# A second group of seven products in each gate/up pair, with two of its weight sums made in DRAM

## The chip, the cores and the metric

The kernel runs on one core of a Trainium2 chip. The metric is device time in microseconds (us) of one launch. The kernel before takes 2517.18 us, the median of three runs from 2516.54 to 2518.18 us. All arithmetic is float32 in the sense that every matrix product is built from reduced-precision parts, as described below.

## The reference, cut to what matters

Two layers on 256 tokens with a width of 2048. The first layer is a Mamba-2 mixer, the second is attention with forget gates; each is followed by the same feed-forward block, and that block is what the change is about:

```
def swiglu(h, w_gate_up, w_down):
    g, u = jnp.split(h @ w_gate_up, 2, axis=-1)
    return (jax.nn.silu(g) * u) @ w_down
...
h = h + swiglu(rmsnorm(h, ffn_norm_w[layer]), w_gate_up[layer], w_down[layer])
```

`h` is 256 x 2048, `w_gate_up` is 2048 x 11264 (gate and up, 5632 columns each), `w_down` is 5632 x 2048, all float32. Each of the two layers has its own weights, so the block runs twice.

## The kernel before, in words

**Tiling.** Every weight is cut into blocks of 512 columns, and each block into groups of 512 rows (a k group: four k tiles of 128 rows, 1 MB). The 256 tokens are two halves of 128. For one k tile and one token half, TensorE does three products into the same PSUM bank: high part of the activation by high part of the weight, high by low, low by high. So a k group of one block costs 4 x 2 x 3 = 24 matmuls of 128x512, and of a pair of blocks (one gate block and its up block) 48.

**Splitting weights.** A loaded weight tile (`wraw`) is split by two engines: ScalarE writes the rounded high part (`whi`, `split_hi`, line 260), VectorE writes the remainder (`wlo`, `split_lo`, line 266). One such step, two k tiles by 512 columns, is called a piece here; it feeds 12 matmuls. There are four buffers each of `whi` and `wlo` (`SPL`), and the pieces are split three ahead of the one that TensorE multiplies, so the high part of a piece waits until TensorE has finished the piece four before it.

**Pairs and seven products.** `pair` (line 320) builds two blocks that share their activations. In the k groups named by `crossed`, the 2x2 arrangement (two token halves, two k tiles by two blocks) is computed with seven products in place of eight, by sums of weights and sums of activations: 7 x 2 x 3 = 42 matmuls in place of 48. The seven are called d, g, a, c, e, b, f. Four are held in PSUM banks of their own (d, a, c, e; tag `mis`, four banks in all), three go straight into the two blocks' accumulators (tag `acc`, also four banks in all). VectorE makes the sums of weights in place in `wraw` (line 384), four additions of 128x1024 per group, between the splits. Afterwards `parts` (lines 677 to 686) combines d, a, c and e on VectorE, `gate` adds them to the left block's accumulators and applies SiLU, and `up` does the same with the right block, multiplies, and transposes the result into an activation slot.

**Order around the change.** A feed-forward block has eleven gate/up pairs; each has four k groups, and k group 2 is the crossed one. The order within a pair is left 0, left 1, right 0, right 1, the seven products of group 2, left 3, right 3. A pair's left accumulators are the banks that the next pair's left block takes first.

**Planner.** Everything but the matmul stream (`parts`, `gate`, `up`, transposes, the mixers) is a task that `Flow` advances at points between matmuls, when its own clock says that its inputs are ready and that ScalarE and VectorE are not more than 4 us behind. `finish` places what is left of a task at once: the next pair's left block forces the previous `gate` (lines 493 to 495), and the first product that needs a bank of its own forces all urgent and middle tasks (line 413). Each engine then executes its instructions strictly in the order in which they were placed.

**Loads.** Sync (SP) issues one 1 MB DMA per k group and block into one of three `wraw` buffers (`RAW`), after the last split that reads the buffer. GpSimd (POOL) computes a power for each normalisation (line 526) and issues the mixers' own DMAs (lines 819, 919, 1117, 1120); nothing else.

Of the kernel before, what the change touches and what calls it, by code (L numbers as in the profile page):

```python
# [17 lines left out]
P = 128  # L18
# [21 lines left out]
RAW = 3  # L40
SPL = 4

# [137 lines left out]
class Unit:  # L180


    def __init__(self, blk, kg, src, width, pieces):
        self.blk, self.kg, self.src, self.width, self.pieces = blk, kg, src, width, pieces
        self.raw = None


class Block:
# [3 lines left out]
    def __init__(self, xs, done, fills=None, wcol=None):  # L192
        self.xs, self.done, self.fills, self.wcol = xs, done, fills, wcol
        self.units, self.ps, self.task = [], None, None


class Cross:
# [8 lines left out]
    ORDER = "dgacebf"  # L206

    def __init__(self, left, right, parts):
        self.left, self.right, self.parts, self.ps = left, right, parts, {}


class Group:

# [6 lines left out]
def kernel(ctx: ExitStack, tc: tile.TileContext, xT_d, x_d, cols_d, rows_d, wdt_d, win_d,  # L220
# [84 lines left out]

    def wide(xs, src, done, fills=None, wcol=None):

        b = Block(xs, done, fills, wcol)
        for kg in range(len(xs)):
            b.units.append(Unit(b, kg, src[kg].rearrange("p (k n) -> p k n", n=NB), NB, [[0, 1], [2, 3]]))  # L310
        blocks.append(b)

    def narrow(xs, src, width, done, wcol=None):

        b = Block(xs, done, None, wcol)
        nk, step = KT * len(xs), NB // width
        b.units.append(Unit(b, 0, src, width, [list(range(a, min(a + step, nk))) for a in range(0, nk, step)]))
        blocks.append(b)

    def pair(xs, sources, done, fills, crossed, parts):  # L320


        both = [Block(xs, d, f) for d, f in zip(done, fills)]
        x = Cross(*both, parts)
        order, rights = [], []
        for kg in range(len(xs)):
            us = [Unit(b, kg, src[kg].rearrange("p (k n) -> p k n", n=NB), NB, [[0, 1], [2, 3]])
                  for b, src in zip(both, sources)]
            if kg in crossed:
                order += rights  # L330
                rights = []
                order.append(Group(x, us, xs[kg], kg == crossed[0], kg == crossed[-1]))
            else:
                for b, u in zip(both, us):
                    b.units.append(u)
                order.append(us[0])
                rights.append(us[1])
        blocks.append(order + rights)

# [7 lines left out]
    def load(u, apart=False, before=None):  # L347
        n = sum(len(p) for p in u.pieces)
        u.raw = wraw.tile([P, n, u.width], F32, tag="wraw", name=nm("wraw"))
        for ks in u.pieces if apart else [range(n)]:  # L350
            if before is not None:
                before(ks)
            nc.sync.dma_start(out=u.raw[:, ks[0]:ks[-1] + 1, :], in_=u.src[:, ks[0]:ks[-1] + 1, :])

    def split_piece(u, ks):
        n = len(ks)
        us = n * u.width / 1024
        ready = flow.work("V", 1.14 * us, flow.work("A", 0.95 * us, flow.at["E"]) + LAT)
        raw = u.raw[:, ks[0]:ks[0] + n, :]
        wcol = u.blk.wcol  # L360
        if u.width < NB:
            both = wspl.tile([P, n, 2, u.width], F32R, tag="whi", name=nm("whi"))
            if wcol is not None:
                nc.vector.tensor_tensor(out=raw, in0=raw, op=ALU.mult,
                                        in1=cols[:, wcol + ks[0]:wcol + ks[0] + n].unsqueeze(2).to_broadcast([P, n, u.width]))
            split(both[:, :, 0, :], both[:, :, 1, :], raw)
            return both, None, ready
        hi = wspl.tile([P, n, u.width], F32R, tag="whi", name=nm("whi"))
        lo = wspl.tile([P, n, u.width], F32R, tag="wlo", name=nm("wlo"))
        if wcol is None:  # L370
            split(hi, lo, raw)
        else:
            for i, k in enumerate(ks):
                split(hi[:, i, :], lo[:, i, :], raw[:, i, :], col(wcol + u.kg * KT + k))
        return hi, lo, ready

    def split_cross(x, name):

        (g, u) = (v.raw.rearrange("p (j i) n -> p i j n", i=2) for v in x.units)
        b11, b21, b12, b22 = g[:, 0], g[:, 1], u[:, 0], u[:, 1]  # L380

        def add(out, in0, in1):
            flow.work("V", 1.22, flow.at["E"])
            nc.vector.tensor_tensor(out=out, in0=in0, in1=in1, op=ALU.add)  # L384

        src = {"d": b21, "g": b11, "a": b21, "c": b22, "e": b21, "b": b22, "f": b12}[name]
# [3 lines left out]
        if name == "g":  # L390
            add(b22, b12, b22)
        if name == "c":
            add(b21, b12, b21)
        split_lo(hi, lo, src)
        ready = flow.work("V", 1.22, flow.work("A", 1.05, flow.at["E"]) + LAT)
        if name == "d":
            add(b21, b21, b22)
        if name == "c":
            add(b22, b11, b21)
        return hi, lo, ready  # L400

    def cross_step(group, name, parts):
# [20 lines left out]
        for p in range(2):  # L423
            xh, xl = a_of(0, p), a_of(1, p)
            nc.tensor.matmul(ps, lhsT=xh, rhs=hi[:, p, :], start=group.first and p == 0 and name not in own, stop=False)  # L425
            nc.tensor.matmul(ps, lhsT=xh, rhs=lo[:, p, :], start=False, stop=False)  # L426
            nc.tensor.matmul(ps, lhsT=xl, rhs=hi[:, p, :], start=False, stop=group.last and p == 1 and name not in own)  # L427
        if group.last and name == "e":
            spawn(x.parts(x))
        flow.work("E", STEP)  # L430
        flow.pump()

    def stream(pre_load, pre_split):
        pieces, units = [], []
        for b in blocks:
            for u in b.units if isinstance(b, Block) else b:
                if isinstance(u, Group):
                    pieces += [(u, n) for n in Cross.ORDER]
                    units += u.units
# [4 lines left out]
        loaded = [0]  # L444

        def load_to(n):
            while loaded[0] < min(n, len(units)):
                i = loaded[0]
                if i in pre_load:
                    pre_load[i]()  # L450
                load(units[i], i < 2, load_x0 if i == 0 else None)
                loaded[0] += 1

        def split_to(n):
            for i in range(len(parts), min(n, len(pieces))):
                u, ks = pieces[i]
                if isinstance(u, Group):
                    parts[i] = split_cross(u, ks)
                    if ks in "ef":
                        load_to(units.index(u.units["ef".index(ks)]) + 1 + RAW)  # L460
                    continue
                if i in pre_split:
                    pre_split[i]()
                parts[i] = split_piece(u, ks)
                if ks is u.pieces[-1]:
                    load_to(units.index(u) + 1 + RAW)

        load_to(RAW)
        split_to(SPL - 1)
        held = deque()  # L470
        for i, (u, ks) in enumerate(pieces):
# [8 lines left out]
            if u.width < NB:  # L480
                if b.ps is None:
                    b.ps = bank([2 * u.width, T])
                for j, k in enumerate(ks):
# [13 lines left out]
            last = u is b.units[-1] and ks is u.pieces[-1]  # L497
# [3 lines left out]
            for n, (j, t) in enumerate(order):  # L501
                k = u.kg * KT + ks[j]
# [3 lines left out]
                nc.tensor.matmul(b.ps[t], lhsT=xh, rhs=hi[:, j, :], start=k == 0, stop=False)  # L506
                nc.tensor.matmul(b.ps[t], lhsT=xh, rhs=lo[:, j, :], start=False, stop=False)  # L507
                nc.tensor.matmul(b.ps[t], lhsT=xl, rhs=hi[:, j, :], start=False, stop=k == nk - 1)  # L508
# [3 lines left out]
            if last:  # L512
                b.task = spawn(b.done(b.ps))
                if b.fills is not None:
                    b.fills.task = b.task
# [156 lines left out]
    def ffn_up(xs, r, gu_d, summed):  # L672
# [37 lines left out]
        for nb in range(NFB):  # L710
            x = [None]

            def took(y, x=x):
# [4 lines left out]
                 (None, acts[nb]), (2,), took)  # L718
# [312 lines left out]
    xs2, r2 = out_stage(ys, wout_d, C_F0, WOUT, summed=(2,))  # L1031
# [182 lines left out]
    xs4, r4 = out_stage(oT, wo_d, C_F1, (2,), summed=(2,))  # L1214
# [15 lines left out]
    pre_load = {i: (lambda i=i: load_x(i)) for i in range(4)}  # L1230
    pre_load[5] = late_loads
    pre_load[12] = load_h
# [5 lines left out]
    blocks[0].units[0].pieces = [[0], [1], [2, 3]]  # L1238
# [7 lines left out]
def _blocks(w):  # L1246
# [3 lines left out]
    w = w.reshape(k // 512, KT, P, n // NB, NB)  # L1250
# [13 lines left out]
def _layout(i):  # L1264
# [13 lines left out]
    def gu(w):  # L1278
        g, u = _blocks(w[:, :DFF]), _blocks(w[:, DFF:])
# [10 lines left out]
        "wout": _blocks(i["a_out_proj"][0]),  # L1290
        "gu0": gu(i["w_gate_up"][0]),
        "dn0": _blocks(i["w_down"][0]),
# [4 lines left out]
        "wo": _blocks(i["w_o"][0]),  # L1297
        "gu1": gu(i["w_gate_up"][1]),
        "dn1": _blocks(i["w_down"][1]),
# [21 lines left out]
```

## Time and profile before

| | |
|---|---|
| median of three runs | 2517.18 us |
| profiled execution, its own time | 2517.21 us |
| span in its profile | 2515.4 us |
| TensorE busy | 2502.9 us, 11542 matmuls |
| VectorE busy | 1938.8 us (77%) |
| ScalarE busy | 1370.1 us (54%) |
| DMA moved | 481.11 MB, 191 GB/s over the span |
| granted TensorE clock | 1.00 throughout |

A busy TensorE is one whose matmuls overlap, so busy time alone does not say that it runs at its fastest; the distance from one matmul's start to the next does. The launch takes about 1.8 us beyond the span.

### The profile page before, as it was taken

Reading aid. Unit: us, or ns where it says so; the run is one execution under the profiler, and the core shown is the slowest. Engines: PE = TensorE matmul, PEld = TensorE weight load, DVE = VectorE, ACT = ScalarE, POOL = GpSimd, SP = SyncE. Lnnn points to the kernel's source line nnn. Section 1 sums busy time; section 2 is a strip of 40 time slices with the busy share of each in tenths; the row PEclk is TensorE's granted clock in tenths of the full one; section 3 lists DMA queues with packets and bytes.
Section 4 is the critical chain, followed back from the end, with each engine's and each line's share of the span. In section 5 each row is a group of like instructions: output and inputs, shape, how many; then the busy total and the mean of one; then the engine's idle time right before and its main releaser. Section 6 shows DMA issues by size and latency. Waiting matters only on the chain.

```text
span 2515.4 us, 30043 instructions
## 1 busy us (share of the span) xinstructions
PE 2502.9 (100%) x11542; PEld 2076.0 (83%) x11542; DVE 1938.8 (77%) x2499; ACT 1370.1 (54%) x1733; POOL 39.5 (2%) x52
## 2 busy tenths in 40 slices
PE   9999999999999999999999999999999999999999
PEld 7888888887878888888888888888878888888887
DVE  7777777778788878788767667678887878879767
ACT  6665566555555555455545555655555555555544
POOL 0000000000000000000000000000000000000000
PEclk9999999999999999999999999999999999999999
DMA  7655455445554646465565555444555564645564
GB/s 269 223 175 174 178 182 203 167 168 196 186 203 168 218 167 223 178 217 184 181 216 187 200 175 203 163 168 170 182 182 203 184 215 169 219 167 206 200 230 150
DMA packets 68319, 481.11 MB, mean 191 GB/s; under 512 B 7600, under 2 KB 8256, under 8 KB 10576
## 3 DMA queue, kind: packets, MB, share of 16 engines
q1 hardware_dynamic: 66672, 468.64, 52.5%
q0 software_dynamic: 1504, 10.57, 1.0%
q8 instruction: 90, 1.47, 0.2%
q14 instruction: 53, 0.43, 0.0%
HBM read 477.00 MB, written 2.18 MB: 190 GB/s over the span
## 4 chain that ended last, share of the span: by engine, by line
PE 96%; DVE 3%; DMA 1%; ACT 0%; issue 0%; SPq 0%; ACTq 0%; DVEq 0%
PE acc L506 26%; PE acc L507 26%; PE acc L508 26%; PE mis L426 2%; PE mis L427 2%; PE mis L425 2%; PE acc L425 2%; PE acc L427 2%; PE acc L426 2%; PE mis L539 1%; DVE wlo L266 1%; PE mis L967 1%; DVE wraw L384 1%; PE mis L837 0%; DMA xraw<-in_xT_dram 0%; PE mis L973 0%
## 5 line engine op out<-in xcount | busy, mean ns | idle before, releaser
L266 DVE TENSOR_TENSOR wlo<-wraw,whi 128x1024 fp32r<-128x1024 f32 (+1 forms) x899 | 1079.7, 1220 | 349.1 <-ACT whi L260 341.2
L260 ACT CAST whi<-wraw 128x1024 fp32r<-128x1024 f32 (+1 forms) x902 | 929.4, 1049 | 740.4 <-PE acc L508 544.5
L506 PE MATMUL acc<-whi,xT 128*128 128x512 f32 x2816 | 1107.2, 393 | 0.5 <-ACT whi L260 0.4
L507 PE MATMUL acc<-wlo,xT 128*128 128x512 f32 x2816 | 1097.4, 390 | 1.0 <-DVE wlo L266 0.7
L508 PE MATMUL acc<-whi,xT 128*128 128x512 f32 x2816 | 1097.5, 390 | 0.0
L508 PEld LDWEIGHTS acc<-whi,xT 128*128 128x128 f32 x2816 | 528.9, 188 | 110.8
L507 PEld LDWEIGHTS acc<-wlo,xT 128*128 128x128 f32 x2816 | 529.4, 188 | 109.9 <-DVE wlo L266 2.6
L506 PEld LDWEIGHTS acc<-whi,xT 128*128 128x128 f32 x2816 | 529.3, 188 | 109.1 <-issue 1.2
L268 DVE SCALAR_TENSOR_TENSOR wlo<-wraw,cols,whi 128x512 fp32r<-128x512 f32 x192 | 134.6, 748 | 70.8 <-ACT whi L262 70.3
L262 ACT ACTIVATE whi<-wraw,cols 128x512 fp32r<-128x512 f32 x192 | 127.5, 717 | 72.2 <-PE acc L508 67.1
L384 DVE TENSOR_TENSOR wraw<-wraw,wraw 128x1024 f32<-128x1024 f32 x76 | 93.0, 1224 | 3.3 <-DMA wraw<-in_wout_dram 1.0
L384 DVE TENSOR_TENSOR wraw<-wraw 128x1024 f32<-128x1024 f32 x76 | 93.1, 1225 | 2.6
L426 PE MATMUL mis<-wlo,xS 128*128 128x512 f32 x228 | 89.5, 393 | 4.2 <-DVE wlo L266 4.2
L427 PE MATMUL mis<-whi,xS 128*128 128x512 f32 x228 | 88.7, 389 | 0.0
L425 PE MATMUL mis<-whi,xS 128*128 128x512 f32 x228 | 88.7, 389 | 0.0
L266 DVE TENSOR_TENSOR xT<-mis,xT 128x512 fp32r<-128x512 f32 x52 | 33.5, 686 | 37.2 <-ACT xT L260 37.2
L260 ACT CAST xT<-mis 128x512 fp32r<-128x512 f32 x52 | 27.9, 590 | 53.4 <-PE mis L539 53.4
L425 PE MATMUL acc<-whi,xT 128*128 128x512 f32 x144 | 56.1, 389 | 0.0
L427 PE MATMUL acc<-whi,xT 128*128 128x512 f32 x144 | 56.0, 389 | 0.0
L426 PE MATMUL acc<-wlo,xT 128*128 128x512 f32 x144 | 56.0, 389 | 0.0
L426 PEld LDWEIGHTS mis<-wlo,xS 128*128 128x128 f32 x228 | 42.8, 188 | 15.9 <-DVE wlo L266 7.3
L526 POOL TENSOR_TENSOR rs<-ms,mhalf 128x4 f32<-128x4 f32 (+1 forms) x27 | 30.2, 1119 | 1494.8 <-DVE ms L524 1494.5
(241 smaller groups left out, 1890.7 us busy)
## 6 DMA issues: line engine op xcount, KB each, us to landing
wraw<-in_gu_dram SPq DMA_DIRECT2D x176, 1024.0 KB, 4.9
wraw<-in_dn_dram SPq DMA_DIRECT2D x88, 1024.0 KB, 4.9
wraw<-in_win_dram SPq DMA_DIRECT2D x78, 1024.0 KB, 4.9
wraw<-in_wout_dram SPq DMA_DIRECT2D x32, 1024.0 KB, 5.0
wraw<-in_wq_dram SPq DMA_DIRECT2D x16, 1024.0 KB, 5.0
wraw<-in_wk_dram SPq DMA_DIRECT2D x16, 1024.0 KB, 4.9
wraw<-in_wv_dram SPq DMA_DIRECT2D x16, 1024.0 KB, 4.9
wraw<-in_wo_dram SPq DMA_DIRECT2D x16, 1024.0 KB, 4.9
```

Of the source, the lines that this page charges most:

```text
L260: nc.scalar.copy(out=hi, in_=src)
L262: nc.scalar.activation(hi, src, AF.Copy, scale=scal)
L266: nc.vector.tensor_tensor(out=lo, in0=src, in1=hi.bitcast(F32), op=ALU.subtract)
L268: nc.vector.scalar_tensor_tensor(out=lo, in0=src, scalar=scal, in1=hi.bitcast(F32), op0=ALU.mult, op1=ALU.subtract)
L384: nc.vector.tensor_tensor(out=out, in0=in0, in1=in1, op=ALU.add)
L425: nc.tensor.matmul(ps, lhsT=xh, rhs=hi[:, p, :], start=group.first and p == 0 and name not in own, stop=False)
L426: nc.tensor.matmul(ps, lhsT=xh, rhs=lo[:, p, :], start=False, stop=False)
L427: nc.tensor.matmul(ps, lhsT=xl, rhs=hi[:, p, :], start=False, stop=group.last and p == 1 and name not in own)
L506: nc.tensor.matmul(b.ps[t], lhsT=xh, rhs=hi[:, j, :], start=k == 0, stop=False)
L507: nc.tensor.matmul(b.ps[t], lhsT=xh, rhs=lo[:, j, :], start=False, stop=False)
L508: nc.tensor.matmul(b.ps[t], lhsT=xl, rhs=hi[:, j, :], start=False, stop=k == nk - 1)
L526: nc.gpsimd.tensor_tensor(out=r, in0=ms, in1=mhalf[:, :width], op=ALU.pow)
```

## The change

In ten of the eleven gate/up pairs of each feed-forward block, k groups 1 and 2 are both computed by seven products; in the last pair only group 2, as before. The order within a pair becomes left 0, right 0, group 1, left 3, group 2, right 3, and the order of the seven products f, d, c, a, e, g, b. The four banks of d, c, a and e are held from group 1 to group 2, and the left block is finished with group 2's product b.

Of the sums of weights in these groups, two (b22 + b12 and b22 + b21, 512 KB each) no longer come from VectorE. They are made in DRAM by GpSimd's queue: a DMA copies one part into a DRAM tile, a second DMA adds the other part to it; the group then loads five parts of 512 KB (f, d, c, a, g) in place of two of 1 MB, and VectorE makes the two remaining sums. `next_sum` is called with every eighth load in program order, and also where a load needs a sum that has not been made. All other weights are loaded in units of 512 KB as well, into six buffers in place of three; a buffer is given to the next load when all units before it are dead too. On the host, the k tiles of the paired weights are stored in the order 0, 2, 1, 3, so that a unit is contiguous. The activation sums are made for k groups 1 and 2.

```
-RAW = 3
+RAW = 6
+PACE = 8
...
 def pair(xs, sources, done, fills, crossed, parts, made=False):
...
+            us = [halves(b, kg, src[kg], ([0, 2], [1, 3])) for b, src in zip(both, sources)]
             if kg in crossed:
-                order += rights
-                rights = []
-                order.append(Group(x, us, xs[kg], kg == crossed[0], kg == crossed[-1]))
+                if not (made and kg > crossed[0]):
+                    order += rights
+                    rights = []
+                (b11, b21), (b12, b22) = us
+                if made:
+                    c, a = Sum(b22.src, b12.src), Sum(b22.src, b21.src)
+                    sums.extend((c, a))
+                    first = {"f": b12, "d": b21, "c": Unit(None, kg, c, NB, [1, 3]),
+                             "a": Unit(None, kg, a, NB, [1, 3]), "g": b11}
+                else:
+                    first = {"d": b21, "g": b11, "+": b22, "f": b12}
+                order.append(Group(x, first, xs[kg], kg == crossed[0], kg == crossed[-1]))
...
+        if made and len(crossed) > 1:
+            n = next(i for i in range(len(order) - 1, 0, -1) if isinstance(order[i], Group))
+            both[0].after = order.pop(n)
+            order.append(both[0].after)
         blocks.append(order + rights)
+
+    def next_sum(n=1):
+        for _ in range(n):
+            i = next((i for i, v in enumerate(sums) if not v.made), None)
+            if i is None:
+                return
+            for v in sums[i:i + 2]:
+                if v.tile is None:
+                    v.tile = dram.tile([P, 2, NB], F32, name=nm("wsum"))
+                    nc.gpsimd.dma_start(out=v.tile, in_=v.one)
+            nc.gpsimd.dma_start(out=sums[i].tile, in_=sums[i].other, accum_op=ALU.add)
+            sums[i].made = True
...
+        if group.cross.made:
+            place, dead = {"e": "c", "b": "c"}, {"f": "f", "c": "d", "a": "a", "g": "g", "b": "c"}
+            early, late = {}, {"c": ("c", "c", "d"), "e": ("c", "c", "g")}
...
+        def load_on():
+            while dead[0] < len(units) and units[dead[0]].dead:
+                dead[0] += 1
+            while loaded[0] < min(dead[0] + RAW, len(units)):
                 i = loaded[0]
                 if i in pre_load:
                     pre_load[i]()
-                load(units[i], i < 2, load_x0 if i == 0 else None)
+                if i % PACE == PACE - 1:
+                    next_sum()
+                load(units[i], i == 0, load_x0 if i < 2 else None)
                 loaded[0] += 1
...
-                 (None, acts[nb]), (2,), took)
+                 (None, acts[nb]), (1, 2) if nb < NFB - 1 else (2,), took, made=True)
...
-    xs2, r2 = out_stage(ys, wout_d, C_F0, WOUT, summed=(2,))
+    xs2, r2 = out_stage(ys, wout_d, C_F0, WOUT, summed=(1, 2))
-    xs4, r4 = out_stage(oT, wo_d, C_F1, (2,), summed=(2,))
+    xs4, r4 = out_stage(oT, wo_d, C_F1, (2,), summed=(1, 2))
...
+PAIRED = (0, 2, 1, 3)
```

## Rows read from the trace of the kernel before

**Rows 1.** The page: busy time, share of the span and instructions of each engine.
```profile
PE 2502.9 (100%) x11542; PEld 2076.0 (83%) x11542; DVE 1938.8 (77%) x2499; ACT 1370.1 (54%) x1733; POOL 39.5 (2%) x52
```
**Rows 2.** The page: the chain that ended last, shares by engine.
```profile
PE 96%; DVE 3%; DMA 1%; ACT 0%; issue 0%; SPq 0%; ACTq 0%; DVEq 0%
```
**Rows 3.** Windows of one gate/up pair: length, busy by engine, clock, DMA share, GB/s.
```profile
2028.84:2071.89 43.05, 43.05 (x196) 35.73 (x195) 34.95 (x35) 22.28 (x24) 0.00 (x0) 1.00 0.55 195
...
923.43:966.49 43.06, 43.06 (x197) 35.74 (x195) 34.96 (x35) 22.28 (x24) 0.00 (x0) 1.00 0.55 195
```
**Rows 4.** Timeline of TensorE in that pair: start, length, instruction.
```profile
2043.16 0.39 PE L425 MATMUL mis<-whi,xT 128*128 128x512 f32 x1
...
2052.68 0.39 PE L506 MATMUL acc<-whi,xT 128*128 128x512 f32 x1
...
2063.56 0.39 PE L506 MATMUL acc<-whi,xT 128*128 128x512 f32 x1
```
**Rows 5.** Timeline of VectorE in that pair, from the group's last splits on.
```profile
2046.89 4.77 DVE L266 TENSOR_TENSOR wlo<-wraw,whi 128x1024 fp32r<-128x1024 f32 x4
2051.59 0.68 DVE L622 TENSOR_TENSOR v<-mis,d 128x512 f32<-128x512 f32 x1
2052.30 0.69 DVE L622 TENSOR_TENSOR y<-mis,v 128x512 f32<-128x512 f32 x1
2053.03 0.69 DVE L622 TENSOR_TENSOR v<-mis,v 128x512 f32<-128x512 f32 x1
2053.64 2.35 DVE L266 TENSOR_TENSOR wlo<-wraw,whi 128x1024 fp32r<-128x1024 f32 x2
2055.91 0.68 DVE L622 TENSOR_TENSOR u<-v,mis 128x512 f32<-128x512 f32 x1
2056.50 2.35 DVE L266 TENSOR_TENSOR wlo<-wraw,whi 128x1024 fp32r<-128x1024 f32 x2
2059.41 1.23 DVE L266 TENSOR_TENSOR wlo<-wraw,whi 128x1024 fp32r<-128x1024 f32 x1 [0.55 <-ACT whi L260]
2060.55 0.68 DVE L622 TENSOR_TENSOR d<-acc,d 128x512 f32<-128x512 f32 x1
2061.15 0.68 DVE L622 TENSOR_TENSOR y<-acc,y 128x512 f32<-128x512 f32 x1
```
**Rows 6.** Groups by line: busy us, mean ns, idle before, releaser.
```profile
L384 DVE TENSOR_TENSOR wraw<-wraw 128x1024 f32<-128x1024 f32 x76 | 93.1, 1225 | 2.6
L260 ACT CAST whi<-wraw 128x1024 fp32r<-128x1024 f32 (+1 forms) x902 | 929.4, 1049 | 740.4 <-PE acc L508 544.5 <-DVE wraw L384 56.5 <-DMA wraw<-in_gu_dram 48.1
```
**Rows 7.** Waits: who waited for whom, us in total, times, longest.
```profile
PE mis L426 <- DVE wlo L266: 4.2, 6, 0.9
```
**Rows 8.** DMA issues of the whole span: KB each, median us to landing.
```profile
wraw<-in_gu_dram SPq DMA_DIRECT2D x176, 1024.0 KB, 4.9
...
e<-acT_d POOLq DMA_DIRECT2D x8, 1024.0 KB, 5.5
...
wraw<-in_wdt_dram SPq DMA_DIRECT2D x1, 512.0 KB, 3.6
```
**Rows 9.** Windows where both queues, then GpSimd's alone, have packets; columns as in rows 3.
```profile
118.50:119.30 0.80, 0.80 (x5) 0.65 (x5) 0.80 (x2) 0.00 (x0) 0.00 (x0) 1.00 1.04 410
119.30:123.50 4.20, 4.20 (x20) 3.49 (x19) 2.56 (x4) 3.02 (x4) 0.00 (x0) 1.00 1.01 427
```
**Rows 10.** DMA queues between 118.5 and 119.3 us: packets, MB, share of 16 engines.
```profile
q1 hardware_dynamic: 36, 0.20, 61.1%
q0 software_dynamic: 15, 0.12, 42.5%
```
**Rows 11.** Timeline of GpSimd: its last set-up instruction, and two powers, 694.94 us apart.
```profile
2.33 0.29 POOL L293 TENSOR_SCALAR_AFFINE_SELECT amask<-amask 128x128 f32<-128x128 f32 x1
...
723.34 1.60 POOL L526 TENSOR_TENSOR rs<-ms,mhalf 128x2 f32<-128x2 f32 x1 [176.18 <-DVE ms L524]
1419.87 0.69 POOL L526 TENSOR_TENSOR rs<-ms,mhalf 128x2 f32<-128x2 f32 x1 [694.94 <-DVE ms L524]
```

More of the change, by code (lines that the diff above doesn't have):

```diff
@@ L180, with __init__ @@
 class Unit:
-    def __init__(self, blk, kg, src, width, pieces):
-        self.blk, self.kg, self.src, self.width, self.pieces = blk, kg, src, width, pieces
-        self.raw = None
+    def __init__(self, blk, kg, src, width, ks, step=2):
+        self.blk, self.kg, self.src, self.width, self.ks = blk, kg, src, width, ks
+        self.pieces = [list(range(a, min(a + step, len(ks)))) for a in range(0, len(ks), step)]
+        self.raw, self.dead = None, False
+class Sum:
+    def __init__(self, one, other):
+        self.one, self.other, self.tile, self.made = one, other, None, False
 class Block:
@@ L193, in __init__ @@
         self.xs, self.done, self.fills, self.wcol = xs, done, fills, wcol
-        self.units, self.ps, self.task = [], None, None
+        self.units, self.ps, self.task, self.after = [], None, None, None
 class Cross:
-    ORDER = "dgacebf"
-    def __init__(self, left, right, parts):
-        self.left, self.right, self.parts, self.ps = left, right, parts, {}
+    def __init__(self, left, right, parts, made):
+        self.left, self.right, self.parts, self.made, self.ps = left, right, parts, made, {}
+        self.order = "fdcaegb" if made else "dgacebf"
 class Group:
@@ L315, in narrow, with pair @@
         b = Block(xs, done, None, wcol)
-        nk, step = KT * len(xs), NB // width
-        b.units.append(Unit(b, 0, src, width, [list(range(a, min(a + step, nk))) for a in range(0, nk, step)]))
+        b.units.append(Unit(b, 0, src, width, list(range(KT * len(xs))), NB // width))
         blocks.append(b)
-    def pair(xs, sources, done, fills, crossed, parts):
+    def pair(xs, sources, done, fills, crossed, parts, made=False):
         both = [Block(xs, d, f) for d, f in zip(done, fills)]
-        x = Cross(*both, parts)
+        x = Cross(*both, parts, made)
@@ L426, in cross_step, with finish_block @@
             nc.tensor.matmul(ps, lhsT=xh, rhs=lo[:, p, :], start=False, stop=False)
-            nc.tensor.matmul(ps, lhsT=xl, rhs=hi[:, p, :], start=False, stop=group.last and p == 1 and name not in own)
+            stop = name in "gb" and x.left.after is group if name in own else group.last
+            nc.tensor.matmul(ps, lhsT=xl, rhs=hi[:, p, :], start=False, stop=stop and p == 1)
         if group.last and name == "e":
             spawn(x.parts(x))
+        if name == "b" and x.left.after is group:
+            finish_block(x.left)
         flow.work("E", STEP)
         flow.pump()
+    def finish_block(b):
+        b.task = spawn(b.done(b.ps))
+        if b.fills is not None:
+            b.fills.task = b.task
     def stream(pre_load, pre_split):
@@ L496, in stream @@
                 b.ps = [acc.tile([P, u.width], F32, tag="acc", name=nm("acc")) for _ in range(NT)]
-            last = u is b.units[-1] and ks is u.pieces[-1]
+            last = b.after is None and u is b.units[-1] and ks is u.pieces[-1]
             order = [(j, t) for j in range(len(ks)) for t in range(NT)]
@@ L1237 @@
     pre_split[8] = lambda: stat.append(spawn(stats()))
-    blocks[0].units[0].pieces = [[0], [1], [2, 3]]
+    blocks[0].units[0].pieces = [[0], [1]]
     warm = bank([P, P])
```

123 lines of the change are left out of this document (61 added, 62 removed).

## The prediction, made before the changed kernel was run

> **What bounds the kernel now.** I read the page's busy times first: TensorE is busy for 2502.9 of 2515.4 us [rows 1]. That alone proves little, because its matmuls overlap, so the chain of waits comes next: 96% of it runs over TensorE [rows 2]. Then the windows of single gate/up pairs, two from different feed-forward blocks: each takes 43.05 us with TensorE without a gap, VectorE busy 34.95 us and ScalarE 22.28 [rows 3]. The timeline gives the price of one matmul: from the group's first product at 2043.16 to the first matmul behind it at 2052.68 are 42 matmuls, 9.52 us, 0.2267 each; the next 48 end at 2063.56, 10.88 us, the same price [rows 4]. So the feed-forward blocks are bound by the number of matmuls. But VectorE is at 81% there, in strict order, and its work comes in bursts. That, and what a new DMA stream does to the loads, decides what the change is worth.
>
> All sums are made against the profiled execution, 2517.2 us (span 2515.4 and 1.8 of launch); the median shown is the same.
>
> **What goes.** Ten pairs in each of two blocks compute one more group with 42 matmuls in place of 48: 20 x 6 x 0.2267 = 27.2 us off TensorE. Nothing is added to it: transposes and all other products stay. If nothing else ended last, a pair would take 43.05 - 1.36 = 41.69 us.
>
> **VectorE and ScalarE.** A plain group needs four splits, a crossed one seven, so each of the 20 pairs gets three more: 3 x 1.05 us on ScalarE [rows 6], which goes to 25.4 of 41.7 us and is no bound. On VectorE three at 1.22. The additions stay four per pair: two groups with two each, against one with four. VectorE goes to 34.95 + 3.66 = 38.6 of 41.7 us, 93%. It fits on average; the question is where it is late.
>
> The place is the seam between two pairs. The next pair's left block writes the banks that `gate` reads, so its first matmul waits for `gate`'s first addition. Before, a left piece pair lies between the group and the end (group, left 3, right 3), and that addition stands at 2060.55, done at 2061.2, 2.3 us ahead of the matmul at 2063.56 [rows 4, 5]. After, only right 3 follows group 2. I walk VectorE's order from the moment t = 0 when TensorE has finished group 2's f. The high part of e waits for f's buffer (that ScalarE mostly waits for TensorE's buffers is the 544.5 us in [rows 6]), so e's remainder starts at 1.1. Then, in the order in which rows 5 shows the same kinds of work, VectorE has: seven remainders (e, g, b, right 3 twice, next left 0 twice) at 4.70/4 = 1.175 from start to start, 8.2 us; one addition of weights at 1.22 [rows 6]; the four combinations of `parts` at 0.71, 0.73, 0.61 and 0.59, 2.64 us; `gate`'s first addition, 0.68 [rows 5]. That ends at 1.1 + 8.2 + 1.2 + 2.6 + 0.7 = 13.8 us. TensorE meanwhile has six products at 1.36 and right 3 at 5.44, 13.6 us. It is late by 0.2, and 0.1 for the signals between engines: I take 0.3 us for each of 20 seams, 6 us. Bounds: nothing, if `parts` falls a little earlier in the order; and 1.2 us each (24 us) if the six additions go at their full 0.70 with waits between them.
>
> **Entry of the blocks.** Before, the first crossed group of a block comes after eight pieces, now after four, and what is left of the stage ahead (transposes, splits, sums of activations, now for one k group more) is forced in there. The crossed products' waits for VectorE at such places come to 4.2 us in six [rows 7]. I add 2 us for each of the two blocks, 4 us; bounds 0 and 8.
>
> **The loads.** A pair now loads 18 units of 512 KB, 9.44 MB in 42 us, 225 GB/s, against 195 [rows 3]. The engines have shown 427 GB/s with a full queue [rows 9], so the stream fits. Half-size loads lose some: a 512 KB load landed after 3.6 us, a 1 MB one after 4.9 [rows 8]. The six buffers hold what three held. One cover gets thin: unit c lives until product b is split, so the next pair's second, third and fourth load start only then, at about 1.1 + 4 x 1.175 + 0.05 = 5.9 us of the walk above, and the second lands at 9.5. Its remainder is due at about 12.0, its cast 1.05 earlier: 1.4 us of cover. It costs nothing alone; any delay of that load above 1.4 us goes straight into the seam.
>
> The Trainium skill says under "Rules for kernel authors" of DMA: Bandwidth & Descriptors that full bandwidth wants 1 MiB or more per DMA, which speaks against 512 KB loads. By it the thin cover would shrink; by the landing times above, in which no run has yet shown a stream of half-size loads, it holds.
>
> **The sums in DRAM.** 42 groups (20 pairs with two, two last pairs with one) have 84 sums, 168 DMAs of 512 KB. No row shows a copy from DRAM to DRAM or an adding DMA. Below, each costs what a load's data costs, 0.524 MB at 427 GB/s, 1.23 us of all engines, 207 us over the kernel. Above, counting passes over DRAM by that price, a copy reads and writes (2 x 1.23), an adding DMA reads twice and writes (3 x 1.23). I take the lower end, as the nearest rows are plain transfers of GpSimd's queue at full rate [rows 9], and keep the upper for the range.
>
> Calls are spread over every eighth load in program order, but what paces them on the chip is GpSimd's own order. It waits for nothing but its copies until its next power, and after the power at 723.34 the next one is 694.94 us later [rows 11]. Counting units (161, 64, 197, 88 in the first four stages), 28 calls lie ahead of the first feed-forward block and 36 between those two powers. So these 36 are not spread: GpSimd runs them off one behind the other at the start of the first block, where loads are densest. When both queues have packets they share: in 0.8 us q1 moved 0.20 MB and q0 0.12, together at 410 GB/s [rows 9, 10]. By even turns of equal packets the loads get 212 of the 225 GB/s that they need, for 36 x 2 x 1.23 x 2 = 177 us; GpSimd's wait for a copy before it adds leaves gaps, in which loads recover. I take 3 us for thin covers (four pairs, under 1 us each). At the start GpSimd is free at 2.6 us [rows 11], so the first copies run while the first loads do: two copies and one add, 3.7 us of the engines; half of it on the path, 2 us.
>
> **Sum.** 2517.2 - 27.2 + 6 + 4 + 3 + 2 = 2505 us. Its own range, from seams at nothing and no contention (2492) to seams at 0.6 (2512).
>
> **Rivals.**
> A, the burst starves the loads. Place: the first block's start. Let a packet of the sums cost x load packets. Each of the 16 engines has 36 x 2 x 8 = 576 such packets of 4 KB, and in turns lets as many of the loads through, 37.7 MB, which lasts TensorE 168 us at 225 GB/s. The burst takes 576 x 0.154 x (1 + x): at x = 1, 177 us; at 1.5, 222; at 2.5 (copies 2, adds 3), 310. TensorE falls behind by 9, 54 and 142 us, less 13 us of loads in the buffers. It decides from x = 1.2 on, where the 27 us begin to go: at 1.5 the kernel takes about 2505 - 3 + 41 = 2543, at 2.5 about 2631, and smaller bursts (eight calls between GpSimd's powers ahead of this one, some five behind the last) come on top. For it: nothing holds GpSimd back, and TensorE has no slack. Against it: sharing was seen for parts of a us only, and the engines are at 55% otherwise [rows 3].
> The Trainium skill gives 207 to 214 GB/s for copies between HBM tensors ("Latency and other measured facts", DMA: Bandwidth & Descriptors), about half of what loads reach here. No row here shows such a copy; by that figure a copy is at x = 2, so the page speaks for this rival.
> B, VectorE becomes the bound. Seams at 1.2 us, and entries at 4: 2517.2 - 27.2 + 24 + 8 = 2522, less what overlaps: no change, about 2518. For it: 93% busy, and the 13.8 against 13.6. Against: in rows 5 the short additions already go at 0.60 where nothing is dependent.
> C, the additions in DRAM leave VectorE idle enough that the seams vanish: 2495. It is inside the first range.
>
> **Chances.** The forecast with C 0.53, B 0.13, A 0.34 (half of it under 2560). Differences under 0.2%, 5 us, can't be told from no change: faster 0.54, same 0.12, slower 0.34. The likeliest time is 2505 us; the range for 8 in 10 goes from 2491 to 2585, which leaves out A's upper end.
>
> **What would show it.** Right: pairs of 42.0 us in the second block, 120 fewer 512-wide matmuls in all, TensorE idle only at the seams, ended by VectorE's `gate` (line with d<-acc,d). Wrong: pairs of 43 us there (B); or a first block whose pairs start at 50 us and more, with ScalarE waiting for `wraw` landings from `in_gu_dram` or `wsum` and GpSimd's DMAs packed behind 723 us (A). If the DMAs of GpSimd lie spread over the whole span, my reading of its order is wrong.

## The result, and the profile after

The changed kernel takes 2599.26 us (median of four runs, 2598.14 to 2601.74) against 2517.24 us: ratio 1.0327, 95% interval 1.0309 to 1.0345. It is slower by 82 us, where 2505 us, 12 less than before, was forecast. Its profiled execution has a span of 2597.1 us, 81.7 longer than before.

The page of the kernel after, its busy times, queues and chain:

```profile
PE 2516.7 (97%) x11422; PEld 2064.6 (79%) x11422; DVE 2009.7 (77%) x2575; ACT 1437.3 (55%) x1805; POOL 153.6 (6%) x220
...
q1 hardware_dynamic: 135792, 490.69, 56.0%
q0 software_dynamic: 25696, 98.66, 14.5%
...
PE 77%; DVE 9%; DMA 8%; ACT 3%; issue 2%; SPq 0%; ACTq 0%; DVEq 0%
```

120 matmuls are gone, as forecast, yet TensorE is busy longer [rows 1], and its share of the chain falls from 96% to 77% [rows 2]; DMA, 1% before, now has 8%. Windows of the kernel after tell where: the stretch behind the power at the first block's start, the block's first two pairs, and a pair of the second block.

```profile
740.00:975.00 235.00, 203.20 (x795) 155.41 (x794) 160.28 (x156) 106.84 (x113) 49.07 (x73) 0.92 1.03 326
784.60:842.60 58.00, 48.16 (x189) 35.95 (x188) 38.90 (x38) 25.84 (x28) 12.05 (x18) 0.94 1.04 331
842.60:900.30 57.70, 49.80 (x189) 37.66 (x188) 39.17 (x39) 26.38 (x28) 12.08 (x18) 0.88 1.05 331
...
2158.70:2201.10 42.40, 41.99 (x189) 34.54 (x188) 38.20 (x39) 25.12 (x27) 0.00 (x0) 1.00 0.67 223
```

In the second block a pair takes 42.38 us, against 43.05 [rows 3]: there the change gains. In the first block the pairs, from one transpose of the activations to the next, take 58.0, 57.7, 55.8 and 50.6 us before they settle at 42.38. In these pairs the DMA share is 1.04 (0.55 in rows 3), and GpSimd is busy. Its timeline in the kernel after:

```profile
740.07 0.71 POOL L581 TENSOR_TENSOR rs<-ms,mhalf 128x2 f32<-128x2 f32 x1 [147.08 <-DVE ms L579]
740.76 0.59 POOL L377 DMA_DIRECT2D wsum<-in_gu_dram  x1
741.33 0.86 POOL L378 DMA_DIRECT2D wsum<-in_gu_dram  x1
...
753.29 0.81 POOL L378 DMA_DIRECT2D wsum<-in_gu_dram  x1 [6.31 <-DMA wsum<-in_gu_dram]
753.83 0.80 POOL L377 DMA_DIRECT2D wsum<-in_gu_dram  x1
...
965.25 0.82 POOL L378 DMA_DIRECT2D wsum<-in_gu_dram  x1 [4.72 <-DMA wsum<-in_gu_dram]
1497.28 0.71 POOL L581 TENSOR_TENSOR rs<-ms,mhalf 128x2 f32<-128x2 f32 x1 [531.20 <-DVE ms L579]
```

L377 is the copy, L378 the adding DMA. All 36 calls between two powers run in one burst of some 230 us, each add waiting only for its copy, and then GpSimd has nothing to do for 531 us: what the prediction read from [rows 11], but with a cost that it put at 3 us. The DMA queues of the kernel after from 760 to 960 us (packets, MB, share of 16 engines; issues with the median us to landing):

```profile
q0 software_dynamic: 8988, 32.75, 61.6%
q1 hardware_dynamic: 9125, 33.22, 42.6%
...
wsum<-in_gu_dram POOLq DMA_DIRECT2D x64, 512.0 KB, 11.1
wraw<-in_gu_dram SPq DMA_DIRECT2D x47, 512.0 KB, 16.5
wraw<-wsum SPq DMA_DIRECT2D x14, 512.0 KB, 16.5
```

The two queues move packets in nearly equal numbers (8988 and 9125), but a packet of the sums costs 0.616 x 200 x 16 / 8988 = 219 ns of an engine and one of the loads 149 ns. So the loads get 33.22 MB in 200 us, 166 GB/s, where a pair brings 9.44 MB: 9.44 / 0.166 = 57 us, the length of the slow pairs. A load lands after 16.5 us there, 5.2 over the whole span.

### The profile page after: what moved, and what is told of

The parts are those of the page before. It is cut to its first block, busy times and chain, and to the rows that moved or that the text cites. A ratio compares the mean times of both kernels' runs of the same rounds, so it can differ in the third digit from the quotient of the medians.

```text
span 2597.1 us, 31677 instructions
## 1 busy us (share of the span) xinstructions
PE 2516.7 (97%) x11422; PEld 2064.6 (79%) x11422; DVE 2009.7 (77%) x2575; ACT 1437.3 (55%) x1805; POOL 153.6 (6%) x220
## 3 DMA queue, kind: packets, MB, share of 16 engines
q8 instruction: 90, 1.47, 0.2%
## 4 chain that ended last, share of the span: by engine, by line
PE 77%; DVE 9%; DMA 8%; ACT 3%; issue 2%; SPq 0%; ACTq 0%; DVEq 0%
PE acc L562 20%; PE acc L563 20%; PE acc L564 20%; DVE wlo L276 5%; DMA wraw<-wsum 5%; ACT whi L270 2%; DMA wraw<-in_gu_dram 2%; PE mis L475 2%; PE mis L476 2%; PE mis L478 2%; PE acc L476 2%; PE acc L478 2%; PE acc L475 2%; DVE wraw L429 2%; PE mis L594 1%
## 5 line engine op out<-in xcount | busy, mean ns | idle before, releaser
L276 DVE TENSOR_TENSOR wlo<-wraw,whi 128x1024 fp32r<-128x1024 f32 (+1 forms) x959 | 1150.1, 1220 | 370.0 <-ACT whi L270 361.0
L270 ACT CAST whi<-wraw 128x1024 fp32r<-128x1024 f32 (+1 forms) x962 | 990.6, 1049 | 757.3 <-PE acc L564 417.8
L562 PE MATMUL acc<-whi,xT 128*128 128x512 f32 x2496 | 986.7, 395 | 32.2 <-DVE d L677 25.0
L563 PE MATMUL acc<-wlo,xT 128*128 128x512 f32 x2496 | 977.3, 392 | 3.5 <-DVE wlo L276 3.3
L564 PE MATMUL acc<-whi,xT 128*128 128x512 f32 x2496 | 976.4, 391 | 0.0
L562 PEld LDWEIGHTS acc<-whi,xT 128*128 128x128 f32 x2496 | 471.1, 189 | 137.5 <-issue 34.6
L563 PEld LDWEIGHTS acc<-wlo,xT 128*128 128x128 f32 x2496 | 471.5, 189 | 103.9 <-DVE wlo L276 8.6
L564 PEld LDWEIGHTS acc<-whi,xT 128*128 128x128 f32 x2496 | 470.9, 189 | 99.0
L429 DVE TENSOR_TENSOR wraw<-wraw,wraw 128x1024 f32<-128x1024 f32 x148 | 181.3, 1225 | 10.5 <-DMA wraw<-in_wout_dram 4.1
L475 PE MATMUL mis<-whi,xS 128*128 128x512 f32 x348 | 141.9, 408 | 16.8 <-ACT y L614 8.3
L478 PE MATMUL mis<-whi,xS 128*128 128x512 f32 x348 | 140.9, 405 | 0.0
L476 PE MATMUL acc<-wlo,xT 128*128 128x512 f32 x224 | 88.7, 396 | 8.7 <-DVE wlo L276 8.7
L475 PEld LDWEIGHTS mis<-whi,xS 128*128 128x128 f32 x348 | 68.3, 196 | 35.9 <-ACT y L614 9.2
L378 POOL DMA_DIRECT2D wsum<-in_gu_dram x84 | 70.5, 839 | 317.5 <-DMA wsum<-in_gu_dram 317.2
L478 PE MATMUL acc<-whi,xT 128*128 128x512 f32 x224 | 87.8, 392 | 0.0
L475 PE MATMUL acc<-whi,xT 128*128 128x512 f32 x224 | 87.7, 392 | 0.0
L478 PEld LDWEIGHTS mis<-whi,xS 128*128 128x128 f32 x348 | 68.4, 197 | 14.2
```

The lines of the kernel that those rows point to most:

```text
L270: nc.scalar.copy(out=hi, in_=src)
L276: nc.vector.tensor_tensor(out=lo, in0=src, in1=hi.bitcast(F32), op=ALU.subtract)
L378: nc.gpsimd.dma_start(out=sums[i].tile, in_=sums[i].other, accum_op=ALU.add)
L429: nc.vector.tensor_tensor(out=us[out].raw, in0=us[in0].raw, in1=us[in1].raw, op=ALU.add)
L562: nc.tensor.matmul(b.ps[t], lhsT=xh, rhs=hi[:, j, :], start=u is b.units[0] and ks[j] == 0, stop=False)
```

## The experiments

Two theories stood at first: the burst (the sums' DMAs, bunched, take the loads' turns) and the loads of 512 KB by themselves. What remained of the error without sums was then split into the seams between pairs and the entry of the blocks. Diffs are against the changed kernel unless said otherwise; all were timed in three rounds beside the kernel before, which took 2517.22 us beside the first four, 2518.47 beside the next four, and 2517.78 beside the last. Pair lengths are distances between transposes as above; stage lengths are distances between GpSimd's powers.

**Sums paced.**

```
+    pace = const.tile([P, 1], F32, name="pace")
...
                 if i % PACE == PACE - 1:
+                    nc.gpsimd.tensor_tensor(out=pace, in0=units[dead[0]].raw[:, 0, 0:1], in1=mhalf[:, :1], op=ALU.mult)
                     next_sum()
```

> The changed kernel with one GpSimd instruction of 128x1 ahead of each of the spread calls, which reads the oldest weight tile not yet dead, so that GpSimd cannot run ahead of the loads. Theory burst (the sums' DMAs run off in bulk and starve the loads): the pairs of the first block go from 56-58 us to 42.4-43.5, GpSimd's DMAs lie spread, the start loses no 7.7 us; 2530 us, 2518 to 2545. Theory small loads (512 KB loads are late by themselves): nothing changes, 2590 to 2600. Theory VectorE (the added splits and seams are the loss): nothing changes either.

Measured: 2542.03 us (2541.02 to 2544.08), ratio 1.0098 (1.0083 to 1.0113). The timeline of GpSimd in the paced kernel:

```profile
752.96 1.10 POOL L513 TENSOR_TENSOR pace<-wraw,mhalf 128x1 f32<-128x1 f32 x1 [13.63 <-DMA wraw<-in_gu_dram]
...
773.06 0.19 POOL L513 TENSOR_TENSOR pace<-wraw,mhalf 128x1 f32<-128x1 f32 x1 [17.66 <-DMA wraw<-in_gu_dram]
```

One call now follows the next after some 20 us instead of 6.5. The same DMAs, moved in time only, cost 57 us less: pairs are 42.4, but for one of 44.3 and one of 45.3. It is at the slow end of the expectation because places other than the block still collide: against the run without sums, the output stage takes 185.2 us instead of 175.2, the start 4.8 us more, and the first block with its down projection 704.1 instead of 696.2.

**No sums made.**

```
-            while not src.made:
-                next_sum()
-            src = src.tile
+            src = src.one
...
-                if i % PACE == PACE - 1:
-                    next_sum()
```

> The changed kernel without any copy or adding DMA: units c and a are loaded straight from the first summand (so these two sums are left out of the result's arithmetic); matmuls, splits, loads in number and size are the same. Theory burst: all that the DMAs cost goes, the pairs of both blocks take 42.4 us, 2517 less 20 x 0.67, plus two entries at some 5 us: 2514, 2506 to 2524. Theory small loads: above 2570. Theory VectorE: above 2570.

Measured: 2520.90 us (2517.5 to 2522.95, ten runs), ratio 1.0013 (1.0004 to 1.0022). So the sums' DMAs cost 2599.3 - 2520.9 = 78 us of the 82. By stages of the profiled executions: 7.7 us at the start, 11.1 in the output stage ahead of the block, 61.0 in the first block and its down projection, 1.8 at the end. But it is 7 us above the 2514 expected, so something else is late too. A pair of its second block, then a stretch at that block's entry, in windows of the kernel without sums:

```profile
2035.00:2077.30 42.30, 41.88 (x189) 34.48 (x188) 38.12 (x39) 25.14 (x27) 0.00 (x0) 1.00 0.68 224
...
1817.00:1827.20 10.20, 5.95 (x13) 4.30 (x14) 6.42 (x16) 7.33 (x18) 0.70 (x1) 0.52 0.14 53
```

and the waits of TensorE in it, over the whole span:

```profile
PE mis L473 <- ACT y L610: 8.3, 2, 4.2
PE acc L558 <- DVE d L673: 8.2, 20, 0.4
PE mis L473 <- DVE xT L278: 3.5, 2, 1.7
```

At each block's entry TensorE idles 4.16 and 1.74 us for activations and their sums (`y`, `xT`), ahead of GpSimd's power. During the first of these waits the granted clock falls to the lower of its levels, 1.2 GHz, and stays there for 3.4 us in the first block and 10.2 in the second (mean 0.52 in the window). What this costs can be read between points that stand at the same place in the matmul stream: from the power before each block's own to the block's first transposes. The kernel before, first and second block:

```profile
546.10:751.06 204.96, 202.19 (x905) 165.32 (x903) 168.89 (x194) 111.73 (x141) 2.66 (x2) 1.00 0.54 195
1419.87:1859.18 439.31, 436.01 (x2074) 362.93 (x2073) 328.77 (x582) 254.73 (x434) 23.09 (x21) 1.00 0.51 179
```

The kernel without sums:

```profile
546.10:757.56 211.46, 204.39 (x911) 167.36 (x910) 177.37 (x209) 118.50 (x151) 1.75 (x2) 0.99 0.58 194
1417.53:1865.84 448.31, 439.29 (x2074) 364.84 (x2073) 337.28 (x597) 261.79 (x444) 22.26 (x21) 0.99 0.54 177
```

The first stretch is 6.5 us longer, of which six more matmuls are 1.4; the second is 9.0 us longer with the same matmuls; 0.7 us of each is the first seam. So the entries lose 4.4 and 8.3 us. The 8.5 and 9.9 us of the expectations further on are another reading: from the block's own power to the transposes are 36.3 and 40.2 us, against 27.7 and 30.3 before. But the power stands earlier in the stream there, and 158 and 166 matmuls lie in these stretches in place of 115 and 126, so that difference is not the loss. The profiled execution is the fastest of the ten, with a mean granted clock of 0.997; the others have 0.995 or 0.996, so part of the 3.4 us from it to the median is clock.

And 20 seams wait 0.41 us each for `gate`'s addition.

**Copies in place of adds.**

```
-            nc.gpsimd.dma_start(out=sums[i].tile, in_=sums[i].other, accum_op=ALU.add)
+            nc.gpsimd.dma_start(out=sums[i].tile, in_=sums[i].other)
```

> The changed kernel with each adding DMA replaced by a plain copy of the second summand (the sum is left out). Theory burst with adds at twice a load packet's price and copies at once: the burst of 36 calls shrinks from 230 to about 180 us, its pairs from 57 to 44-47 us, GpSimd's queue from 14.5% of the engines to about 9.5%; 2545 us, 2530 to 2560. Rival, copies inside DRAM cost double (half the rate of loads) as adds do: little changes, 2580 to 2600, share 13% or more.

Measured: 2552.84 us (2551.24 to 2553.53), ratio 1.0140 (1.0123 to 1.0157). The pairs at the front of the first block take 48.0, 47.5, 47.5 and 43.9 us. The queue's line on the page of this kernel, and its first slow pair:

```profile
q0 software_dynamic: 25696, 98.66, 10.6%
...
773.90:821.90 48.00, 44.61 (x189) 35.37 (x188) 38.47 (x39) 25.39 (x27) 9.24 (x18) 0.96 1.01 390
```

The share gives the two prices, as means over all packets: a DMA of 512 KB has 144 packets here, 128 of 4 KB and 16 of under 512 B. Without sums the queue has 1504 packets and 1.2% of 16 x 2515.6 us, 483 us. Here (0.106 x 16 x 2549.8 - 483) / 24192 = 159 ns for a copy's packet; in the changed kernel (0.145 x 16 x 2597.1 - 483) / 24192 = 229 ns over both kinds, so 299 for an adding one, if the copies there cost what they cost here. For 512 KB that is 1.43 us of all engines for a copy and 2.69 for an add; the prediction had 1.23 for either at its lower end, 2.46 and 3.69 at its upper. Against the 149 ns of a load's packet in the burst, counted in the same way, copies cost 1.07 and adds 2.01, together x = 1.54; the burst itself has 219 / 149 = 1.47. Even near the price of loads, a burst costs 24.6 us in this stage (720.86 against 696.24), and the DMAs for sums cost 2552.8 - 2520.9 = 32 us in all: of 390 GB/s the loads get half, 195, and need 224.

**Loads of 512 KB alone**, in the kernel before (the diff is against that one; with it go the host's k-tile order and the buffers' release):

```
-RAW = 3
+RAW = 6
...
-            b.units.append(Unit(b, kg, src[kg].rearrange("p (k n) -> p k n", n=NB), NB, [[0, 1], [2, 3]]))
+            b.units += halves(b, kg, src[kg], ([0, 1], [2, 3]))
```

> The kernel before with only the loads changed: units of 512 KB in six buffers, paired weights stored as 0, 2, 1, 3; one crossed group per pair, all four sums by VectorE, no DRAM sums. Theory burst and theory VectorE: the loads alone cost nothing, 2513 to 2521. Theory small loads: a good part of the 82 us is here, above 2540.

Measured: 2516.53 us (2515.94 to 2517.54, ten runs), ratio 0.9997 (0.9988 to 1.0006); every pair is 43.05 as before. Small loads cost nothing here.

**The seam.** The run without sums, with the left block's last group cut around group 2:

```
-            both[0].after = order.pop(n)
-            order.append(both[0].after)
+            order.insert(len(order) - 2, order.pop(n))
```

> As the run without the sums' DMAs (the two sum tiles are loaded from the first summand alone, so the products c, a and e, b use other weights), with one more edit: the left block's last k group is cut in two, one half ahead of group 2 and one behind it, and the left block ends with that half, so that a left and a right piece lie between the gate's end and the next pair. Theory 'VectorE is late at the seam' (0.69 us per pair was measured, 42.37 against 41.69): a walk of the three engines in order, with the durations of the trace, has no stall left; pairs fall to 41.7 us and 20 x 0.67 = 13 us go: 2507 us (2504-2511). Rival 'the 0.69 us is not the gate's addition but the heavier VectorE load over the whole pair': pairs stay at 42.2 to 42.4, 2519-2522.

Measured: 2507.04 us (2505.82 to 2507.29), ratio 0.9954 (0.9937 to 0.9970), as the first theory had it. A pair of the second block, window of this kernel:

```profile
2028.10:2069.80 41.70, 41.70 (x190) 34.62 (x189) 38.01 (x39) 25.05 (x27) 0.00 (x0) 1.00 0.68 228
```

VectorE's work is the same 38.0 us, but TensorE has no gap: the loss was where the addition stands, not how much VectorE does.

**The entry.** The run without sums, with the first pair of each block crossed in group 2 alone:

```
-                 (None, acts[nb]), (1, 2) if nb < NFB - 1 else (2,), took, made=True)
+                 (None, acts[nb]), (1, 2) if 0 < nb < NFB - 1 else (2,), took, made=True)
```

> As the run without the sums' DMAs, with one more edit: in the first pair of each of the two blocks only k group 2 is crossed, as in the kernel before; nine pairs a block keep two groups. Theory 'crossing k group 1 at once at the entry is too early for what the stage ahead still owes' (8.5 and 9.9 us lost there, clock halved behind it for 3.4 and 10.2 us): the entries come back, less the 2 x 1.36 us of matmuls that the two pairs then keep: 2520.9 - 18.4 + 2.7 = 2505 us (2501-2510). Rival 'the entry loses its time to the one more summed k group of the output stage (wout, wo with groups 1 and 2)', which stays: the entries stay late, 2519-2524.

Measured: 2502.56 us (2501.74 to 2505.39), ratio 0.9940 (0.9925 to 0.9954). The waits for `y` and `xT` are gone, and 18.3 us come back although two pairs keep 2.7 us of matmuls. The window from the output stage's end to the first transposes of the second block, in this kernel:

```profile
1768.00:1851.00 83.00, 82.37 (x372) 67.83 (x371) 71.35 (x86) 48.66 (x64) 0.70 (x1) 1.00 0.60 200
```

TensorE is idle for 0.6 us of it, at full clock. Both k groups of activation sums are still made in the output stage, so the rival falls: it is the early use of group 1's sums that was late. Over the two stretches shown for the run without sums this kernel takes 203.06 and 438.20 us, 1.9 and 1.1 less than the kernel before; why it is quicker than that was not tried.

**All together, with sums.** Paced sums at chosen loads, each copy one call ahead of its add, and the two edits above:

```
-PACE = 8
+CALLS = {*range(24, 161, 5), *range(233, 360, 10), *range(421, 509, 8), *range(512, 606, 4), *range(650, 720, 10)}
...
-            for v in sums[i:i + 2]:
+            primed = sums[i].tile is not None
+            for v in sums[i:i + 2] if primed else sums[i:i + 1]:
...
+            if not primed:
+                return
...
-                if i % PACE == PACE - 1:
+                if i in CALLS:
+                    nc.gpsimd.tensor_tensor(out=pace, in0=units[dead[0]].raw[:, 0, 0:1], in1=mhalf[:, :1], op=ALU.mult)
                     next_sum()
```

> The whole computation: DRAM sums paced by a GpSimd instruction that reads a live weight tile before each call, the calls put at units where the two feed-forward blocks' loads are not the densest, each copy a call ahead of its adding DMA, the left block's last group cut in two, and the first pair of each block with one crossed group. If burst, seams and entries are the whole loss, they add: 2505 (entries) - 13 (seams), and up to 8 us for contention: 2496 us (2490-2508), faster than the kernel before by 0.4 to 1.0%. If pacing still leaves 1 us of late loads per call (84 calls), 2520-2545 as in the paced run.

Measured: 2495.18 us (2494.85 to 2495.70), ratio 0.9908 (0.9894 to 0.9923). It beats both kernels. Windows of this kernel, the first pair of the first block and a later one beside which sums are made:

```profile
748.90:797.60 48.70, 45.57 (x201) 36.66 (x200) 39.56 (x40) 25.92 (x28) 6.05 (x9) 1.00 0.76 244
881.00:922.70 41.70, 41.70 (x189) 34.62 (x188) 38.10 (x39) 25.02 (x27) 3.98 (x6) 1.00 0.84 271
```

At a DMA share of 0.84 the paced sums cost the later pair nothing. The first stretch has 201 matmuls where later ones have 189: twelve at 0.2267 are 2.7 us, so 4.3 of its 7.0 us more are lateness. Two other pairs of that block take 41.9 and 42.5. As each block's first pair has one group less here, 80 sums are made, not 84.

**The calls moved out of that pair** (diff against the version just shown):

```
-CALLS = {*range(24, 161, 5), *range(233, 360, 10), *range(421, 509, 8), *range(512, 606, 4), *range(650, 720, 10)}
+CALLS = {*range(24, 161, 5), *range(262, 360, 8), *range(421, 509, 8), *range(512, 606, 4), *range(650, 720, 10)}
```

> The whole computation, as in the version that adds the edits, with one difference: the 13 calls for sums that it makes between loads 233 and 353 (about every tenth) lie between loads 262 and 358 (every eighth), so that none falls into the entry and the first pair of the first feed-forward block. That pair took 48.72 us there, 41.70 in the pairs behind it, with ScalarE waiting 5.4, 3.7 and 1.4 us for weights and sums to land; the run without sums lost 2.0 us in the same place. Theory 'copies and adding DMAs beside the refill of the buffers make the loads late': some 5 us come back, 2490 us (2487-2493). Rival 'the first pair is late whatever the calls, and the same calls closer together cost as much elsewhere': 2494-2498.

Measured: 2492.72 us (2491.51 to 2493.40), ratio 0.9900 (0.9884 to 0.9917). Half of the expected 5 us came: the first pair falls from 48.7 to 44.6 us, but the next three take 42.3, 42.9 and 41.9. With its twelve more matmuls 44.4 us is what the first pair needs, so what it was late is back; the 45.1 us of the run with the mended entry and no sums, called a loss of 2.0 us in the expectation, are these matmuls and a seam. Both theories hold in part. This is the fastest version.

**All sums on VectorE**, and with them no call for sums:

```
-        x = Cross(*both, parts, made)
+        x = Cross(*both, parts, False)
...
-                if made:
+                if False:
```

> The changed kernel with no DMA for sums: both crossed groups of a pair make all four sums of weights on VectorE (with the order of products of before), everything else as in the change. It asks what the DRAM sums buy. VectorE has 34.95 + 3.66 + 4 x 1.22 = 43.5 us of work in a pair of 41.7: theory 'VectorE would be the bound': pairs of 43.5 to 44.5 us, 2517 + 20 x (0.5 to 1.5) + 18 for the entries = 2545-2565. Rival 'VectorE has room for two more additions': pairs of 42.4 to 43, 2520-2535.

Measured: 2576.96 us (2574.11 to 2580.22), ratio 1.0233 (1.0218 to 1.0249), beyond the slower theory's range. A pair of the second block, window of this kernel:

```profile
1950.50:1995.40 44.90, 42.79 (x188) 34.35 (x188) 42.45 (x43) 25.51 (x28) 0.00 (x0) 1.00 0.55 187
```

VectorE is busy for 42.45 of 44.9 us and pairs take 44.4 to 45.8 us nearly everywhere, more than the 43.05 before; against the run without sums the whole is 56 us slower, and entries that are later still are part of that. So with all sums on VectorE this version has no gain. That VectorE's work alone is the cause is not shown: the order of the seven products differs too, and in this window VectorE waits 0.98 and 0.37 us for two loads.

## Why the prediction was wrong, point by point

**The step that failed** is "The sums in DRAM", where it takes the lower end of the price and from it "3 us for thin covers". The burst of 36 calls was read rightly from [rows 11], and rival A priced it at x = 1.5, close to what was measured. Even turns of packets are not in [rows 10], which has 36 packets beside 15; they were assumed, and that came out.

Two things in the step were wrong. The first is the price: the plain transfers of [rows 9] were the right neighbour for a copy (1.07) and the wrong one for an adding DMA (2.01), and 2599.3 - 2552.8 = 46 us of the loss are the difference. The second is the overlap: with copies alone, near the price that it took, 32 us are lost, 24.6 of them in this stage, and not 3. The gaps in which the loads were to recover are not there: each call issues the next sum's copy ahead of its own add, and the two queues together fill the engines (61.6% and 42.6%). And the engines moved 390 GB/s in place of 427, so the loads got 195 GB/s where the prediction gave them 212.

The Trainium skill's 207 to 214 GB/s for copies between HBM tensors (DMA: Bandwidth & Descriptors, "Latency and other measured facts"), measured there on rows of 16 KiB, would have put a copy at x = 2. The copies here, in rows of 4 KB, cost 1.43 us of all engines for 0.524 MB, 366 GB/s. The measurement decides: the page's figure is too dear for these copies, and rival A is right for another reason, the adds.

**Rival A's size.** It said 41 us for the block at x = 1.5; 61.0 were measured. Its burst of 222 us came out near 230. Two terms fail. It credited 13 us of loads in the buffers, and nothing of that shows: the rate alone accounts for the whole loss, (57.9 - 42.4) / 57.9 x 230 = 62 us. And the engines moved 331 GB/s where its prices made 427 x 2 / 2.5 = 342. Why the buffers gave no credit was not tried. Part of TensorE's time there is spent at the lower clock (mean 0.92 over 235 us); as the loads' rate accounts for the pair's length, the clock need not add to it. Its "smaller bursts on top" are 11.1 us in the output stage and 1.8 at the end.

**The start.** 2 us forecast, 7.7 measured. The chain of the kernel after (start, length, link) has one landing there, one in the output stage, and twelve between 752 and 967 us; three of them:

```profile
7.97 18.04 DMA wraw<-in_win_dram
...
584.97 17.49 DMA wraw<-in_wout_dram
...
795.13 14.82 DMA wraw<-wsum
```

In the first 30 us a load of 512 KB lands after 13.3 us on the median, and after 7.6 in the run without sums: there is no small burst where the loads are dense. GpSimd issued three copies and two adds there, not two and one.

**The matmuls.** 27.2 us off TensorE was right: with the seam mended, pairs are 41.70 us, as the prediction had them at 41.69.

**The seams.** Place and cause were right, 0.3 us was too little: 0.69 (42.38 - 41.69), 13.8 us in all. TensorE and VectorE at one seam of the kernel after:

```profile
2175.94 0.39 PE L475 MATMUL mis<-whi,xT 128*128 128x512 f32 x1
...
2190.11 0.47 PE L562 MATMUL acc<-whi,xT 128*128 128x512 f32 x1 [0.41 <-DVE d L677]
```

```profile
2189.28 0.68 DVE L677 TENSOR_TENSOR d<-acc,d 128x512 f32<-128x512 f32 x1
```

From the end of f (2175.94) the addition ends at 14.02, not 13.8; the next matmul starts 0.15 later, at 14.17 against the due 13.6, and the first matmuls behind the gap are themselves some 0.1 longer. Each term of the walk was small and each fell on the late side.

**The entries.** 2 us each forecast, 4.4 and 8.3 measured without sums. The prediction bounded them by short waits of [rows 7]; what was late was a longer chain (transpose, ScalarE's `y`, VectorE's differences, two splits) forced for one more k group by the first product that needs a bank, and in the 4.2 us in which TensorE was idle the clock fell.

**The sum, remade:** 2517.2 - 27.2 + 13.8 + 12.7 = 2516.5, against 2517.5 for the profiled execution without sums and 2520.9 for the median, which ran at a lower mean clock; 78 us of sums make 2599. The 1.0 us between stays open.

**The loads.** That 512 KB units fit was right: the Trainium skill's advice of 1 MiB or more per DMA ("Rules for kernel authors", DMA: Bandwidth & Descriptors) does not bind here: the kernel before runs at a ratio of 0.9997 with half the size. **Rival B** falls: VectorE at 38.0 of 41.7 us is no bound. With all sums its own, at 42.5, pairs no longer gain. **Rival C** falls with the seams; VectorE has more to do in a pair than before, 38.0 us against 34.95.

## What to carry to other kernels

A DMA queue without a dependency runs ahead of the place where the program issues it; ask what paces it on the chip, and if nothing does, cost the whole burst at the densest loads beside it, with the dearest packet that it may have. When a forecast lists a mechanism with its own arithmetic and a price that no row shows, take a price inside the bounds, not the end that leaves the gain standing. And where work per group rises on the engine next to the bound, look at the first use and the last use in the loop: both losses outside the DMAs lay there. Reordering won back the one, and one crossed group less in the first pair the other.

## What the runs showed of the hardware

- In the changed kernel an adding DMA of 512 KB from DRAM to DRAM costs 2.69 us of all engines (299 ns an engine per packet), a copy 1.43 (159 ns), in the same queue and at the same sizes; the first figure takes the copies at the price that they have without adds.
- Two queues with packets waiting moved nearly equal numbers of packets for 200 us on end (8988 and 9125, at 219 and 149 ns each), so the cheaper queue is slowed to the rate of the dearer one.
- 168 DMAs of 512 KB for sums cost 78 us bunched and 21 us paced by a 128x1 GpSimd instruction. The 160 of the fastest version cost an estimated 3 to 4 us, if the two edits add: without sums it would take 2520.9 - (2520.9 - 2507.0) - (2520.9 - 2502.6) = 2488.7, or 2490 with the two seams that both edits mend counted once, against 2492.7.
